# Stick-breaking attention: the running products alone go through the value product, and the values are shifted by one token through DRAM

## The chip, the cores and the metric

The kernel runs on one core of a Trainium2 chip. A time is the device time of one launch in microseconds (us), from the first instruction to the last; lower is better. The engines are PE (TensorE, matrix products), DVE (VectorE), ACT (ScalarE), POOL (GpSimd) and SP (SyncE, which here only issues DMAs). Each runs its own instructions strictly in the order in which they stand, and waits at the head of its queue until what the instruction needs has been signalled.

## The reference, cut to what matters

One layer of an encoder over 1024 tokens and 1024 channels: an RMS norm, a projection to four parts (pooling, q, k, v), a causal pooling mixer, stick-breaking attention with 8 heads of 64 channels, gates, an output projection, and an MLP. The change is in the attention:

```python
z = einsum('bhqd,bhkd->bhqk', qb, kb) * scale
mask = arange(t1)[None, :] < arange(t0, t1)[:, None]          # strictly causal: s < t
log_1mb = where(mask, log_sigmoid(-z), 0.0)
tail = cumsum(log_1mb, axis=3, reverse=True) - log_1mb
attn = where(mask, exp(log_sigmoid(z) + tail), 0.0)
out = einsum('bhqk,bhkd->bhqd', attn, vb)
```

So A[t,s] = sigmoid(z_ts) times the product of sigmoid(-z_tj) over s < j < t. With S[t,s] for the product of sigmoid(-z_tj) over s <= j < t, and S = 1 for s >= t, this is a difference of neighbours: A[t,s] = S[t,s+1] - S[t,s].

## The kernel before, in words

Everything is in float32 precision: an operand is split in a rounded high part and a rest (`hi`, `lo`), and a product is three matmuls (`mm3`, lines 115 to 117; 113 is the first of them where it is pinned behind an attention instruction). The program is written as one stream; a scheduler then sets the order of each engine's queue, and tile pools (memory that is handed on) set which instruction must wait for which.

`phase_in` normalises x, makes the pooling part (`pool_group` on DVE, `pool_mix` with a small product `dm` on PE, ACT line 427, DVE line 428, and two stores `yscr<-win` and `yscr<-u` by POOL), and the q and k of heads 0 and 1. Its work tiles lie in a pool `in_b`, which is released at its end.

`phase_attention` then takes over that memory for its pools `att` (the rows T, the split `ahi`, `alo`) and `att_s` (`self.sp`, small staging tiles). For each head, `att_scores` makes eight rows of 128 queries, from the widest (1024 keys) to the narrowest, in pieces of up to 512 keys: scores `z` in one of three PSUM buffers, F = sigmoid(-z) and T = sigmoid(z) by ACT (565, 566), a causal mask on T by POOL (568), a running product of F from right to left by DVE (574), and T times the neighbouring F by DVE (578). `att_steps` transposes T (591) in blocks, splits it by ACT and DVE (599, 600), and multiplies with the values (616) into the PSUM tile `o`; every value tile holds, per head, 64 channels of hi and 64 of lo, so the two halves of `o` are added at the end (625 by ACT, 627 by DVE).

Between these PE works off fillers, pieces of other jobs: gates (`dg`), later q and k (`dqk`), and the values (`dv`, `job_v`, 24 matmuls per tile of 128 tokens, first for heads 0 to 3 as soon as head 0 begins, tokens from the last tile to the first; then for heads 4 to 7 during heads 3 and 4, first tile to last). All fillers share two PSUM buffers (`dps`, tag `d`), in the order written: tile n needs the buffer of tile n-2 back. A value tile's buffer is given back when ACT (508) and DVE (509) have written the value tile in SBUF, which has a pool of its own (`vp`).

DMAs issued by SP load weights (line 79), one weight ahead, and make the swapped copies of q (485). POOL stores the gates and adds up weights for the MLP in DRAM (`wscr`).

Of the kernel before, what the change touches and what calls it, by code (L numbers as in the profile page):

```python
# [52 lines left out]
class Block:  # L53
# [118 lines left out]
    def build(self):  # L172
        tc, nc = self.tc, self.nc
# [315 lines left out]
    def job_v(self, grp):  # L489
        nc = self.nc  # L490
        w = [self.weights(("v", grp, j), 1 - j) for j in range(2)]

        for t in range(NK) if grp else range(NK - 1, -1, -1):
# [12 lines left out]
            dd = d[:, :256].rearrange("p (h x) -> p h x", h=4)  # L506
            r = self.rcol[:, t : t + 1]
            nc.scalar.activation(v[:, :, 0:64], dd, AF.Copy, scale=r)
            nc.vector.scalar_tensor_tensor(
                out=v[:, :, 64:128], in0=dd, scalar=r, in1=v[:, :, 0:64].bitcast(F32), op0=ALU.mult, op1=ALU.subtract  # L510
            )
            self.v[(grp, t)] = v

    def job_gate(self, i, h):
        nc = self.nc
# [22 lines left out]
    def att_scores(self, h, i):  # L538

        nc = self.nc
        p, j = h // 2, h % 2
        q, qs, k = self.qk[("q", p)][j], self.qk[("qs", p)][j], self.qk[("k", p)][j]
        w = (i + 1) * P
        tl = self.tp.tile([P, w], F32, name="T", tag=f"T{i}", bufs=1)
        f = self.tp.tile([P, 1024], F32, name="F", tag="F", bufs=1)
        tt = slice(i * P, i * P + P)  # L550
        past = self.past[:, 1024 - w :]

        low = min(H, w - 2 * P) if w > H else 0
        for c, n in ((low, w - low), (0, low)):
            if n == 0:
                continue
            top = c == low
            cols = slice(c, c + max(256, n))
            z = self.zps.tile([P, H], F32, name="z", tag="z", bufs=3)
            zz = z[:, : max(256, n)]  # L560
            m = nc.tensor.matmul(zz, q[:, tt], k[:, cols], start=True, stop=False)  # L561
# [3 lines left out]
            nc.scalar.activation(f[:, c : c + n], z[:, :n], AF.Sigmoid, scale=-1.0)  # L565
            nc.scalar.activation(tl[:, c : c + n], z[:, :n], AF.Sigmoid)
            if top:
                self.masked = nc.gpsimd.affine_select(  # L568
                    out=tl[:, w - P : w], in_=tl[:, w - P : w], pattern=[[-1, P]], compare_op=ALU.is_gt, fill=0.0,
                    base=0, channel_multiplier=1,  # L570
                )

            fr = f[:, c : c + n][:, ::-1]
            nc.vector.tensor_tensor_scan(  # L574
                fr, fr, past[:, c : c + n][:, ::-1], 1.0 if top else f[:, c + n : c + n + 1], ALU.mult, ALU.max
            )
            e = c + n - top
            nc.vector.tensor_mul(tl[:, c:e], tl[:, c:e], f[:, c + 1 : e + 1])  # L578
        return tl

    def att_steps(self, h, g, a):

        nc = self.nc
        o = self.zps.tile([P, H], F32, name="o", tag="o", bufs=1)
        for s in range(4 * g + 4):
            r0 = max(0, s - 4 * g)
            at = self.zps.tile([P, H], F32, name="at", tag="at", bufs=2)
            hi = self.tp.tile([P, H], F32R, name="ahi", tag="ahi", bufs=2)
            lo = self.tp.tile([P, H], F32R, name="alo", tag="alo", bufs=2)
            for r in range(r0, 4):  # L590
                t = nc.tensor.transpose(at[:, r * P : r * P + P], a[r][:, s * P : s * P + P], self.eye)  # L591
            self.marks.append(t)
            self.pump(self.w_out)

            c0, c = min(r0, 2) * P, r0 * P
            if r0 == 3:
                nc.gpsimd.memset(hi[:, c0:c].bitcast(F32), 0.0)
                nc.gpsimd.memset(lo[:, c0:c].bitcast(F32), 0.0)
# [3 lines left out]
            self.pending = (h, g, s, o, hi, lo, c0)  # L602
            yield

    def att_products(self):

        nc = self.nc
        if self.pending is None:
            return
        h, g, s, o, hi, lo, c0 = self.pending  # L610
        self.pending = None
        last = s == 4 * g + 3
        hd = (h % 4) * P
        v = self.v[(h // 4, s)].rearrange("p h x -> p (h x)")[:, hd : hd + P]
        for part in (hi, lo):
            t = nc.tensor.matmul(  # L616
                o[:, c0:], v, part[:, c0:], start=s == 0 and part is hi, stop=last and part is lo
            )
        self.marks.append(t)
        if not last:  # L620
            return
        b = 64 * (h % 2)
        for c in (0, 256):
            u = self.sp.tile([P, 256], F32, name="ou", tag="ou", bufs=1)
            nc.scalar.copy(u[64:128, :], o[64:128, c : c + 256])
            at = slice(g * H + c, g * H + c + 256)
            nc.vector.tensor_add(self.oT[h // 2][b : b + 64, at], o[0:64, c : c + 256], u[64:128, :])
# [18 lines left out]
    def phase_attention(self):  # L646
        tc, nc = self.tc, self.nc
# [9 lines left out]
        out = None  # L657
        for h in range(8):
# [9 lines left out]
            for n_row, i in enumerate(ROWS):  # L668
# [723 lines left out]
```

## Time and profile before

| what | value |
|---|---|
| median of 3 runs (lowest to highest) | 1276.06 us (1275.58 to 1276.24) |
| span of the profiled execution | 1274.1 us |
| median less that span | 2.0 us |
| PE busy | 1266.1 us, 99% |
| DVE busy | 924.9 us, 73% |
| ACT busy | 614.6 us, 48% |
| POOL busy | 169.6 us, 13% |

The page has no time of its own for the profiled execution beside its span; what the runs are longer by is start and end around it. A busy PE is a PE with a matmul somewhere in its pipeline: a matmul of 512 columns is listed with 389 ns and the next one starts some 225 ns later, so a pause of up to 0.16 us between two starts does not show as idle time. Attention, with its fillers, lies between about 77 and 450 us of the span.

### The profile page before, as it was taken

To read this page: it belongs to the slowest core of one execution; us is meant where nothing else is said; L and a number is where in the kernel's file an instruction comes from. 1 tells how busy PE (TensorE), PEld (TensorE's weight loads), DVE (VectorE), ACT (ScalarE), POOL (GpSimd) and SP (SyncE) were. 2 spreads that over 40 slices of the span, in tenths; PEclk is the share of its full clock that TensorE was granted. 3 is DMA by queue.
4 is the path that set the end of the run, shared out by engine and by line. 5 is a ranking of instruction groups with operands and counts; after the bars stand their busy time and mean duration, and the time that the engine had idled before them with its cause. 6 is when DMAs were issued, how large, how long until landed. Compare 5 with 4: busy or idle time off the path is not lost.

```text
span 1274.1 us, 16614 instructions
## 1 busy us (share of the span) xinstructions
PE 1266.1 (99%) x6043; PEld 1057.7 (83%) x6043; DVE 924.9 (73%) x1315; ACT 614.6 (48%) x1022; POOL 169.6 (13%) x314
## 2 busy tenths in 40 slices
PE   9999999999999999999999999999999999999998
PEld 6898888889888888888878888888888888888887
DVE  8787688786878747551777988877775655776975
ACT  8235455564555542232456646455454433344452
POOL 1002213221223121100101002212120000001000
PEclk9999999999999999999999999999999999999999
DMA  6254447694686138671529578656559546556551
GB/s 226 67 165 166 146 161 163 138 219 141 124 215 223 67 120 232 198 219 33 182 85 303 183 247 277 219 198 208 199 205 346 193 154 223 189 179 238 199 220 67
DMA packets 75729, 233.70 MB, mean 183 GB/s; under 512 B 8608, under 2 KB 11168, under 8 KB 73472
## 3 DMA queue, kind: packets, MB, share of 16 engines
q1 hardware_dynamic: 48352, 144.04, 33.9%
q0 software_dynamic: 27152, 88.49, 23.7%
q8 instruction: 47, 0.77, 0.2%
q14 instruction: 34, 0.28, 0.1%
q10 hardware_dynamic: 144, 0.13, 0.0%
HBM read 178.10 MB, written 83.89 MB: 206 GB/s over the span
## 4 chain that ended last, share of the span: by engine, by line
PE 94%; DVE 3%; issue 1%; ACT 1%; DMA 1%; POOL 0%; SPq 0%; DVEq 0%; ACTq 0%; POOLq 0%
PE d L116 20%; PE d L117 20%; PE d L115 20%; PE dg L117 4%; PE dg L116 4%; PE dg L113 4%; PE o L616 3%; PE at L591 2%; PE dqk L116 2%; PE dqk L117 2%; PE dqk L113 1%; PE z L564 1%; PE z L561 1%; DVE F L574 1%; PE dv L117 1%
## 5 line engine op out<-in xcount | busy, mean ns | idle before, releaser
L116 PE MATMUL d<-blo,whi 128*128 128x512 f32 (+1 forms) x456 | 172.3, 378 | 0.0
L117 PE MATMUL d<-bhi,wlo 128*128 128x512 f32 (+1 forms) x456 | 171.9, 378 | 0.0
L115 PE MATMUL d<-bhi,whi 128*128 128x512 f32 (+1 forms) x456 | 168.7, 378 | 0.0
L574 DVE TENSOR_TENSOR_SCAN F<-F,past 128x256 f32<-128x256 f32 (+2 forms) x96 | 94.2, 981 | 20.9 <-ACT F L565 20.0
L85 ACT CAST whi<-wraw 128x512 fp32r<-128x512 f32 (+1 forms) x88 | 67.7, 799 | 77.2 <-PE d L116 38.0
L113 PE MATMUL dg<-hT_hi,whi 128*128 128x512 f32 x253 | 101.7, 402 | 0.0
L117 PE MATMUL dg<-hT_hi,wlo 128*128 128x512 f32 x256 | 100.8, 394 | 0.0
L116 PE MATMUL dg<-hT_lo,whi 128*128 128x512 f32 x256 | 100.4, 392 | 0.0
L117 PEld LDWEIGHTS d<-bhi,wlo 128*128 128x128 f32 x456 | 85.8, 188 | 15.9
L116 PEld LDWEIGHTS d<-blo,whi 128*128 128x128 f32 x456 | 85.7, 188 | 15.9
L115 PEld LDWEIGHTS d<-bhi,whi 128*128 128x128 f32 x456 | 85.5, 188 | 16.1
L86 DVE TENSOR_TENSOR wlo<-wraw,whi 128x512 fp32r<-128x512 f32 (+1 forms) x88 | 77.7, 905 | 28.4 <-ACT whi L85 28.3
L116 PE MATMUL d<-b_lo,whi 128*128 128x512 f32 x196 | 76.2, 390 | 0.4 <-DVE b_lo L836 0.4
L115 PE MATMUL d<-b_hi,whi 128*128 128x512 f32 x196 | 75.6, 389 | 0.0
L565 ACT ACTIVATE F<-z 128x256 f32<-128x256 f32 (+2 forms) x96 | 47.2, 493 | 58.8 <-DVE T L578 34.4
L117 PE MATMUL d<-b_hi,wlo 128*128 128x512 f32 x196 | 74.7, 389 | 0.0
L1124 DVE TENSOR_TENSOR wlo<-slots_hi,whi 128x1024 fp32r<-128x1024 f32 x29 | 35.5, 1225 | 53.1 <-ACT whi L1122 53.1
L600 DVE TENSOR_TENSOR alo<-at,ahi 128x512 fp32r<-128x512 f32 (+1 forms) x96 | 52.0, 553 | 29.9 <-ACT ahi L599 28.8
L1122 ACT CAST whi<-slots_hi 128x1024 fp32r<-128x1024 f32 x29 | 30.5, 1052 | 84.5 <-PE d L116 71.5
L599 ACT CAST ahi<-at 128x512 fp32r<-128x512 f32 (+1 forms) x96 | 45.1, 482 | 47.4 <-PE at L591 44.0
L1122 ACT CAST whi<-slots_lo 128x1024 fp32r<-128x1024 f32 x27 | 28.4, 1053 | 73.4 <-PE d L116 59.7
L578 DVE TENSOR_TENSOR T<-T,F 128x255 f32<-128x255 f32 (+3 forms) x96 | 53.1, 556 | 11.0 <-POOL T L568 2.5
(323 smaller groups left out, 3309.3 us busy)
## 6 DMA issues: line engine op xcount, KB each, us to landing
wraw<-w SPq DMA_DIRECT2D x80, 512.0 KB, 4.3
wscr<-w POOLq DMA_DIRECT2D x24, 1024.0 KB, 10.0
ext_b<-ascr SPq DMA_DIRECT2D x40, 512.0 KB, 4.3
gscr<-gs POOLq DMA_DIRECT2D x32, 256.0 KB, 4.2
gate<-gscr POOLq DMA_DIRECT2D x16, 512.0 KB, 4.5
pscr<-p SPq DMA_DIRECT2D x32, 256.0 KB, 3.2
braw<-w SPq DMA_DIRECT2D x16, 512.0 KB, 5.1
ascr<-c POOLq DMA_DIRECT2D x32, 256.0 KB, 5.0
```

Of the source, the lines that this page charges most:

```text
L85: nc.scalar.copy(hi[:, c], raw[:, c])
L86: self.last_lo = nc.vector.tensor_sub(lo[:, c], raw[:, c], hi[:, c].bitcast(F32)).ins
L113: nc.tensor.matmul(ps, wh, rh, start=first and i == 0, stop=False)
L115: nc.tensor.matmul(ps, wh, rh, start=first and i == 0, stop=False)
L116: nc.tensor.matmul(ps, wh, rl, start=False, stop=False)
L117: nc.tensor.matmul(ps, wl, rh, start=False, stop=last and i == n - 1)
L565: nc.scalar.activation(f[:, c : c + n], z[:, :n], AF.Sigmoid, scale=-1.0)
L574: nc.vector.tensor_tensor_scan(fr, fr, past[:, c : c + n][:, ::-1], 1.0 if top else f[:, c + n : c + n + 1], ALU.mult, ALU.max)
L578: nc.vector.tensor_mul(tl[:, c:e], tl[:, c:e], f[:, c + 1 : e + 1])
L599: nc.scalar.copy(hi[:, c:], at[:, c:])
L600: nc.vector.tensor_sub(lo[:, c:], at[:, c:], hi[:, c:].bitcast(F32))
L1122: last_split[0] = nc.scalar.copy(hi, src).ins
```

## The change: what it does

`att_scores` makes only sigmoid(-z), straight into the row T, and runs the product over it in place. The second sigmoid, the mask and the multiplication with the neighbour are gone, and F with them. The rows that are transposed now hold S instead of A; masked places hold 1.

The difference is moved to the values: over a row of keys up to the end E of its block, sum of A[t,s] v[s] = v[E-1] + sum of S[t,s] (v[s-1] - v[s]), with v[-1] = 0. `job_v` therefore evicts a value tile with one ACT instruction to a staging tile `vs` (from `att_s`, 2 buffers), SP stores it to DRAM (`vscr`, one zero row ahead of token 0), and `v_steps` loads the same tile shifted by one token (`vb`, 2 buffers), subtracts on DVE, and splits on ACT and DVE. The load of tile t needs the stores of tiles t and t-1; for the first group, which runs from the last tile to the first, `v_steps` of tile t+1 is written behind the eviction of tile t. v[E-1] (`vlast`, 64 channels of 8 heads for 8 blocks) is gathered by four DMAs of single values per group, and is added as the bias of the eviction of `o`, which is cut in halves for that. POOL sets the first token's output to zero. The weight sums are issued two at a time behind POOL's memsets instead of one every second row.

```diff
+        self.vlast = cp.tile([P, 8, NK], F32, name="vlast")
+        nc.vector.memset(self.pad, 0.0)
+        self.vscr = dp.tile([1 + P * NK, H], F32, name="vscr")
+        nc.sync.dma_start(self.vscr[0:1, :].rearrange("o (p n) -> (o p) n", p=P), self.pad[:, 0:4])
...
-            v = self.vp.tile([P, 4, P], F32R, name=f"v{grp}_{t}", tag="v", bufs=9)
-            dd = d[:, :256].rearrange("p (h x) -> p h x", h=4)
-            r = self.rcol[:, t : t + 1]
-            nc.scalar.activation(v[:, :, 0:64], dd, AF.Copy, scale=r)
-            nc.vector.scalar_tensor_tensor(
-                out=v[:, :, 64:128], in0=dd, scalar=r, in1=v[:, :, 0:64].bitcast(F32), op0=ALU.mult, op1=ALU.subtract
-            )
-            self.v[(grp, t)] = v
+            s = self.sp.tile([P, 256], F32, name="vs", tag="vs", bufs=2)
+            nc.scalar.activation(s, d[:, :256], AF.Copy, scale=self.rcol[:, t : t + 1])
+            nc.sync.dma_start(self.vscr[1 + t * P : 1 + t * P + P, cols], s)
+            if grp:
+                self.v_steps(grp, t, s)
+            else:
+                if t < NK - 1:
+                    self.v_steps(grp, t + 1, later)
+                later = s
+        if not grp:
+            self.v_steps(grp, 0, later)
+        for h in range(4 * grp, 4 * grp + 4):
+            nc.sync.dma_start(
+                self.vlast[64:128, h, :], self.vscr[P : P * NK + 1 : P, 64 * h : 64 * h + 64].rearrange("i d -> d i")
+            )
+
+    def v_steps(self, grp, t, s):
+        b = self.sp.tile([P, 256], F32, name="vb", tag="vb", bufs=2)
+        nc.sync.dma_start(b, self.vscr[t * P : t * P + P, 256 * grp : 256 * grp + 256])
+        nc.vector.tensor_sub(b, b, s)
+        bb = b.rearrange("p (h x) -> p h x", h=4)
+        v = self.vp.tile([P, 4, P], F32R, name=f"v{grp}_{t}", tag="v", bufs=9)
+        nc.scalar.copy(v[:, :, 0:64], bb)
+        nc.vector.tensor_sub(v[:, :, 64:128], bb, v[:, :, 0:64].bitcast(F32))
+        self.v[(grp, t)] = v
...
-            nc.scalar.activation(f[:, c : c + n], z[:, :n], AF.Sigmoid, scale=-1.0)
-            nc.scalar.activation(tl[:, c : c + n], z[:, :n], AF.Sigmoid)
-            if top:
-                self.masked = nc.gpsimd.affine_select(
...
-            fr = f[:, c : c + n][:, ::-1]
+            f = tl[:, c : c + n]
+            nc.scalar.activation(f, z[:, :n], AF.Sigmoid, scale=-1.0)
             nc.vector.tensor_tensor_scan(
...
-            e = c + n - top
-            nc.vector.tensor_mul(tl[:, c:e], tl[:, c:e], f[:, c + 1 : e + 1])
...
-            nc.scalar.copy(u[64:128, :], o[64:128, c : c + 256])
+            for j in (0, P):
+                i = (g * H + c + j) // P
+                nc.scalar.activation(
+                    u[64:128, j : j + P], o[64:128, c + j : c + j + P], AF.Identity, bias=self.vlast[64:128, h, i : i + 1]
+                )
...
+        if g == 0:
+            nc.gpsimd.memset(self.oT[h // 2][b : b + 64, 0:1], 0.0)
```

The scheduler's order moves with it. PE has the same number of matmuls, 6033 rows with and without the change. Three places follow, where heads 0 to 3 get their values; line numbers of the changed program are up to 24 higher (565 becomes 589, 427 becomes 431, 421 becomes 425).

On ACT, from the third pooling group to the first sigmoids. `v0_7` is the value tile of tokens 896 to 1023, `v0_6` the one before it; `win` and `ph` belong to the pooling. Before:

```order
L421 CAST ph_742<-win_699 128x1024
L508 ACTIVATE v0_7_924<-dv_899,rcol_165 128x4x64
L508 ACTIVATE v0_6_952<-dv_927,rcol_165 128x4x64
L427 ACTIVATE win_699<-dm_746,vt_150 128x512
L427 ACTIVATE win_699<-dm_752,vt_150 128x512
L508 ACTIVATE v0_5_998<-dv_955,rcol_165 128x4x64
L421 CAST ph_814<-win_769 128x1024
L508 ACTIVATE v0_4_1026<-dv_1001,rcol_165 128x4x64
L508 ACTIVATE v0_3_1054<-dv_1029,rcol_165 128x4x64
L427 ACTIVATE win_769<-dm_818,vt_150 128x512
L427 ACTIVATE win_769<-dm_824,vt_150 128x512
```

The same place in the changed program (`vs_922`, `vs_950`, `vs_995`, `vs_1029` are the evictions of tiles 7, 6, 5 and 4):

```order
L425 CAST ph_818<-win_773 128x1024
L431 ACTIVATE win_773<-dm_822,vt_150 128x512
L431 ACTIVATE win_773<-dm_828,vt_150 128x512
L589 ACT_TABLE_LOAD
L589 ACTIVATE T_878<-z_879 128x512
L589 ACTIVATE T_878<-z_884 128x512
L511 ACTIVATE vs_922<-dv_897,rcol_165 128x256
L511 ACTIVATE vs_950<-dv_925,rcol_165 128x256
L589 ACTIVATE T_984<-z_985 128x384
L589 ACTIVATE T_984<-z_990 128x512
L589 ACTIVATE T_1097<-z_1098 128x256
L534 CAST v0_7_956<-vb_953 128x4x64
```

The evictions of tiles 7 and 6 stood ahead of the last pooling group; they now stand behind it, behind the table load and behind the first two sigmoids. The next eviction (`vs_995`) stands behind the cast of the finished tile 7, and so on down to tile 0: one cast, one eviction.

On PE, just behind the last matmul of `dv` for tile 6. Before:

```order
L561 MATMUL z_982<-k0_776,q0_637 128x384
L564 MATMUL z_982<-k0_776,qs0_736 128x384
L116 MATMUL dm_746<-pq_743,wmh_519 128x512
L117 MATMUL dm_746<-ph_742,wml_520 128x512
L116 MATMUL dm_752<-pq_743,wmh_519 128x512
L117 MATMUL dm_752<-ph_742,wml_520 128x512
L115 MATMUL dv_955<-whi_779,hT_hi1_291 128x256
```

Now:

```order
L117 MATMUL dm_756<-ph_746,wml_524 128x512
L115 MATMUL dm_822<-ph_818,wmh_523 128x512
L115 MATMUL dm_828<-ph_818,wmh_523 128x512
L116 MATMUL dm_822<-pq_819,wmh_523 128x512
L117 MATMUL dm_822<-ph_818,wml_524 128x512
L116 MATMUL dm_828<-pq_819,wmh_523 128x512
L117 MATMUL dm_828<-ph_818,wml_524 128x512
L584 MATMUL z_990<-k0_780,q0_641 128x512
L587 MATMUL z_990<-k0_780,qs0_740 128x512
L584 MATMUL z_1098<-k0_780,q0_641 128x256
L587 MATMUL z_1098<-k0_780,qs0_740 128x256
L115 MATMUL dv_959<-whi_783,hT_hi1_295 128x256
```

The matmuls of the last pooling group and two score pieces now stand between `dv` of tile 6 and of tile 5; before, three tiles of `dv` (72 matmuls) came first. Further on, the remaining score pieces of head 0, three pieces of head 1 and 16 transposes stand between the tiles of `dv`, and all of them stand ahead of the first gate.

On SP, the same group of values. Before, weights and the copies of q alone stood here; now:

```order
L512 DMA vscr_168<-vs_922 128x256
L512 DMA vscr_168<-vs_950 128x256
L530 DMA vb_953<-vscr_168 128x256
L512 DMA vscr_168<-vs_995 128x256
L530 DMA vb_998<-vscr_168 128x256
L512 DMA vscr_168<-vs_1029 128x256
L530 DMA vb_1032<-vscr_168 128x256
L512 DMA vscr_168<-vs_1063 128x256
L530 DMA vb_1066<-vscr_168 128x256
```

Store and load alternate, each load one tile behind the last store.

More of the change, by code (lines that the diff above doesn't have):

```diff
@@ L491, in job_v @@
         w = [self.weights(("v", grp, j), 1 - j) for j in range(2)]
+        cols = slice(256 * grp, 256 * grp + 256)
         for t in range(NK) if grp else range(NK - 1, -1, -1):
@@ L504, in job_v @@
                     yield
-            v = self.vp.tile([P, 4, P], F32R, name=f"v{grp}_{t}", tag="v", bufs=9)
-            dd = d[:, :256].rearrange("p (h x) -> p h x", h=4)
-            r = self.rcol[:, t : t + 1]
-            nc.scalar.activation(v[:, :, 0:64], dd, AF.Copy, scale=r)
-            nc.vector.scalar_tensor_tensor(
-                out=v[:, :, 64:128], in0=dd, scalar=r, in1=v[:, :, 0:64].bitcast(F32), op0=ALU.mult, op1=ALU.subtract
-            )
-            self.v[(grp, t)] = v
+            s = self.sp.tile([P, 256], F32, name="vs", tag="vs", bufs=2)
[12 more added lines that the diff above has]
+                self.vlast[64:128, h, :], self.vscr[P : P * NK + 1 : P, 64 * h : 64 * h + 64].rearrange("i d -> d i")
+            )
+    def v_steps(self, grp, t, s):
+        nc = self.nc
+        b = self.sp.tile([P, 256], F32, name="vb", tag="vb", bufs=2)
[6 more added lines that the diff above has]
+        self.v[(grp, t)] = v
     def job_gate(self, i, h):
@@ L548, in att_scores @@
         tl = self.tp.tile([P, w], F32, name="T", tag=f"T{i}", bufs=1)
-        f = self.tp.tile([P, 1024], F32, name="F", tag="F", bufs=1)
         tt = slice(i * P, i * P + P)
@@ L564, in att_scores @@
             nc.tensor.matmul(zz, qs[:, tt], k[:, cols], start=False, stop=True)
-            nc.scalar.activation(f[:, c : c + n], z[:, :n], AF.Sigmoid, scale=-1.0)
-            nc.scalar.activation(tl[:, c : c + n], z[:, :n], AF.Sigmoid)
-            if top:
-                self.masked = nc.gpsimd.affine_select(
-                    out=tl[:, w - P : w], in_=tl[:, w - P : w], pattern=[[-1, P]], compare_op=ALU.is_gt, fill=0.0,
-                    base=0, channel_multiplier=1,
-                )
-            fr = f[:, c : c + n][:, ::-1]
+            f = tl[:, c : c + n]
+            nc.scalar.activation(f, z[:, :n], AF.Sigmoid, scale=-1.0)
             nc.vector.tensor_tensor_scan(
-                fr, fr, past[:, c : c + n][:, ::-1], 1.0 if top else f[:, c + n : c + n + 1], ALU.mult, ALU.max
-            )
-            e = c + n - top
-            nc.vector.tensor_mul(tl[:, c:e], tl[:, c:e], f[:, c + 1 : e + 1])
+                f[:, ::-1], f[:, ::-1], past[:, c : c + n][:, ::-1], 1.0 if top else tl[:, c + n : c + n + 1],
+                ALU.mult, ALU.max,
+            )
         return tl
@@ L597, in att_steps @@
                 nc.gpsimd.memset(hi[:, c0:c].bitcast(F32), 0.0)
-                nc.gpsimd.memset(lo[:, c0:c].bitcast(F32), 0.0)
+                self.zeroed = nc.gpsimd.memset(lo[:, c0:c].bitcast(F32), 0.0)
             nc.scalar.copy(hi[:, c:], at[:, c:])
@@ L602, in att_steps @@
             self.pending = (h, g, s, o, hi, lo, c0)
+            if s == 4 * g + 3 and h < 7:
+                with self.tc.issue_after(self.zeroed.ins):
+                    next(self.wsums)
+                    next(self.wsums)
             yield
@@ L672, in phase_attention @@
                 self.pump(w_in * share[n_row])
-                if h < 7 and n_row % 2:
-                    with tc.issue_after(self.masked.ins):
-                        next(self.wsums)
                 if h == 0 and n_row < 4:
```

## The prediction

> **What bounds the kernel now.** I read the page first (busy shares, then the chain that ended last), then what PE waited for, then PE's pace in the attention beside a stage of plain matmuls.
>
> ```profile
> PE 1266.1 (99%) x6043; PEld 1057.7 (83%) x6043; DVE 924.9 (73%) x1315; ACT 614.6 (48%) x1022; POOL 169.6 (13%) x314
> PE 94%; DVE 3%; issue 1%; ACT 1%; DMA 1%; POOL 0%; SPq 0%; DVEq 0%; ACTq 0%; POOLq 0%
> ...
> PE at L591 <- DVE T L578: 0.4, 1, 0.4
> ...
> PE o L616 <- DVE oT L627: 0.4, 1, 0.4
> ...
> 100.00:450.00 350.00, 348.85 (x1849) 296.94 (x1849) 275.56 (x433) 195.69 (x422) 82.83 (x156) 1.00 0.59 160
> 500.00:550.00 50.00, 50.00 (x222) 41.40 (x221) 29.80 (x42) 10.86 (x14) 8.50 (x12) 1.00 0.73 196
> ...
> L113 PE MATMUL dg<-hT_hi,whi 128*128 128x512 f32 x253 | 101.7, 402 | 0.0
> L115 PE MATMUL d<-bhi,whi 128*128 128x512 f32 x408 | 155.6, 389 | 0.0
> ```
>
> PE is 94% of the chain. In 350 us of attention it idles 1.15 us (350.00 - 348.85) and waits for the softmax engines for 0.4 us at a time. What short pauses hide in its busy time is seen in the means: the pinned gate matmul is listed 402 ns where plain ones have 389, 13 ns x 253 = 3.3 us. Allowing as much again for `dqk` and the products, all that faster DVE, ACT and POOL work can give back is 0 to 8 us. PE's matmuls are the same in number and shape after the change, so the time can only fall by these pauses, and rises by every new wait of PE.
>
> **What is removed.**
>
> ```profile
> L566 ACT ACTIVATE T<-z x96: 271/504/625, 102.5 to 448.2; 128x512 f32<-128x512 f32 x40, 128x384 f32<-128x384 f32 x24, 128x256 f32<-128x256 f32 x24, 128x128 f32<-128x128 f32 x8
> L578 DVE TENSOR_TENSOR T<-T,F 128x255 f32<-128x255 f32 (+3 forms) x96 | 53.1, 556 | 11.0 <-POOL T L568 2.5
> L568 POOL TENSOR_SCALAR_AFFINE_SELECT T<-T 128x128 f32<-128x128 f32 x64 | 34.8, 544 | 168.9 <-ACT T L566 156.8 <-PE o L616 6.4 <-PE dqk L117 5.6
> L625 ACT COPY ou<-o 64x256 f32<-64x256 f32 x32 | 11.8, 368 | 13.0 <-PE o L616 8.5 <-DVE oT L627 3.9
> ```
>
> 96 x 0.504 = 48 us of ACT, 53 us of DVE, 35 us of POOL; 64 half evictions for 32 cost ACT some 6 us back (64 x 0.28, estimated from 0.368 for twice the width, less 11.8). All of it runs beside PE. I credit 1.5 us of the 0 to 8.
>
> **What is added where the first values are made.** This term carries the sum. ACT, DVE and PE in that stretch, from the timeline:
>
> ```profile
> 84.58 1.22 DVE L405 TENSOR_TENSOR win<-win 128x1022 f32<-128x1022 f32 x1 [1.40 <-DMA yscr<-win]
> 91.64 0.17 DVE L413 TENSOR_TENSOR win<-win,u 128x16 f32<-128x16 f32 x1
> 91.84 1.05 ACT L421 CAST ph<-win 128x1024 fp32r<-128x1024 f32 x1 [1.84 <-DVE win L413]
> 92.91 1.23 DVE L422 TENSOR_TENSOR pq<-win,ph 128x1024 fp32r<-128x1024 f32 x1 [1.11 <-ACT ph L421]
> ...
> 85.36 0.48 ACT L508 ACTIVATE v<-dv,rcol 128x256 fp32r<-128x256 f32 x1 [3.71 <-PE dv L117]
> 96.21 1.27 ACT L427 ACTIVATE win<-dm,vt 128x512 fp32r<-128x512 f32 x2 [0.45 <-PE dm L117]
> 100.73 1.28 ACT L565 ACT_TABLE_LOAD   x1 [0.72 <-DMA yscr<-win]
> 102.03 0.60 ACT L565 ACTIVATE F<-z 128x512 f32<-128x512 f32 x1
> ...
> 85.16 0.34 PE L561 MATMUL z<-k,q 128*128 128x384 f32 x1
> 86.44 0.28 PE L115 MATMUL dv<-whi,hT_hi 128*128 128x256 f32 x1
> 94.96 0.28 PE L117 MATMUL dv<-whi,hT_lo 128*128 128x256 f32 x1
> 95.08 0.63 PE L115 MATMUL dm<-ph,wmh 128*128 128x512 f32 x2
> 122.50 0.60 PE L591 MATMUL at<-eye,T 128*128 128x128 f32 x4
> ```
>
> Before, tiles 7 and 6 are evicted by 85.8. In the changed order their evictions stand behind the table load, which waits for the last pooling store, and two sigmoids. PE now comes to the last `dm` without the 72 `dv` (86.44 to 95.08, 0.12 us each) ahead of it, so that `dm` follows its operands: DVE has two value instructions less on the way, `ph` from about 91.3, `pq` done at 93.6, L427 at 94.2 instead of 96.21. All behind it is 2.0 us earlier: table load 98.7, sigmoids 100.05 to 101.1, evictions of tiles 7 and 6 done at 102.0.
>
> From there every eviction waits for a round trip: eviction, store, load, subtraction, cast, next eviction (two staging buffers, and ACT's order).
>
> ```profile
> L508 ACT ACTIVATE v<-dv,rcol 128x256 fp32r<-128x256 f32 x16 | 7.7, 479 | 12.3 <-PE dv L117 12.1
> L509 DVE SCALAR_TENSOR_TENSOR v<-dv,rcol,v 128x256 fp32r<-128x256 f32 x16 | 7.6, 477 | 3.8 <-ACT v L508 3.8
> out<-ff SPq DMA_DIRECT2D x13, 128.0 KB, 1.8
> pscr<-p SPq DMA_DIRECT2D x32, 256.0 KB, 3.2
> wraw<-w SPq DMA_DIRECT2D x80, 512.0 KB, 4.3
> ...
> L79 SPq DMA_DIRECT2D wraw<-w x4: 327/328/328, 33.0 to 56.1; - x4
> ...
> DMA to landing us min/median/max: 3.4/3.4/3.5
> ```
>
> Eviction and cast 0.48 each, subtraction 0.48. The store is 128 KB like `out<-ff`: 1.8 (upper bound 2.3, between it and twice the size). A load of 128 KB is not in the trace: between 1.8 (the store of its size) and 3.4 (four times the size, alone on the queue); I take 2.2, nearer to the equal size. Four hand-overs, some 0.2. Period 0.48 + 1.8 + 2.2 + 0.48 + 0.48 + 0.2 = 5.6. Six periods lead from tile 6 to tile 0, and in one of them three running products and two splits stand ahead of the subtraction on DVE, +0.8: tile 0 is evicted at 102.0 + 33.6 + 0.8 = 136.4.
>
> The second gate tile needs that buffer. PE's work from 85.16 until there, all in front of it: 144 `dv` x 0.12 = 17.3; 10 `dm` x 0.23 = 2.3 (512 columns: 50 us / 222); 13 score pieces, two matmuls each by their columns, 4.6; 16 transposes at most 0.15 each by the last row above, I take 1.5; the first gate tile, 24 x 0.226 = 5.4. Sum 31.1, so 116.3 without waits. PE waits 136.4 - 116.3 = **20 us**. Nothing covers it: what PE could do instead needs the same two PSUM buffers or the same three score buffers. The products with the last values stand 54 gate matmuls further on (12 us); those values need a last round trip of about 7 us, and PE does not wait for them again. Period 5.0 (load 1.8, no hand-overs) gives 16 us, period 7.3 (load 3.4, store 2.3) 30 us.
>
> By the Trainium skill, "DMA: Bandwidth & Descriptors", section "Anatomy of one DMA — SWDGE (gpsimd) path", a DMA costs about 2.0 us plus its bytes at 436 GB/s, by which store and load would be 2.3 each and the wait about 24 us; the store row above (1.8) is already below it.
>
> **The other added terms.** *Start.* A store of the zero row stands second on SP.
>
> ```profile
> 1.24 0.42 SPq L280 DMA_DIRECT2D vt<-vec  x1
> 3.94 0.18 DVE L281 TENSOR_SCALAR gn<-vt 128x32 f32<-128x32 f32 x1 [2.49 <-DMA vt<-vec]
> ```
>
> Every first load is one issue later, +0.4 (0 to 0.8). *Values of heads 4 to 7.* Here two tiles are in flight (two stores, two loads), so a pair takes about 6.2.
>
> ```profile
> L113 PE MATMUL dv<-whi,hT_hi x64: 278/283/368, 274.2 to 304.3; 128*128 128x256 f32 x64
> wscr<-w POOLq DMA_DIRECT2D x24, 1024.0 KB, 10.0
> SPq L79 <- DVE wlo L86: 454.2, 47, 32.2
> ```
>
> PE spends 30 us on these eight tiles, 7.5 a pair: hidden at 2.2 per load. With the 1 MB sums on the same DMA engines a load may take the 4.3 of the weights, a pair 8.3, and DVE and ACT hold the next rows up while they wait: 0 to 6, I take 1.5. *`vlast`, weight sums, zeroed token.* SP waits 454 us for DVE before weight loads, so a few issues more are hidden; `vlast` lands some 20 us ahead of its first use. 0.
>
> **Sum.** 20 + 0.4 + 1.5 - 1.5 = 20.4 on the profiled span of 1274.1, 1294.5; the median lies 2.0 above that span: **1296 us**.
>
> **Rivals.**
> (A) *The round trip is hidden by an early start.* If the evictions of tiles 7 and 6 kept their place (85.8), six periods would end at 120.2, 4 us of waiting: 1276 + 0.4 + 4 = 1280. For it: the data are there at 85.4. Against: ACT's queue has them behind the table load. 7%.
> (B) *The relief of DVE and ACT wins: faster.* Price: up to 8 us less, in the pauses between pinned matmuls of attention; it decides only if the wait stays below them, which needs (A) and a period under 6: 1276 + 4 - 8 = 1272. Against: PE's waits for these engines are 0.4 us. 4%. The case in between, no change because PE hides both: 3%.
> (C) *PE resumes at a lower pace after each pause.*
>
> ```profile
> 1.43 4.02 PE L313 MATMUL idle<-zero 128*128 128x512 bf16 x9 [1.43 <-DVE zero L310]
> 0.00:5.00 5.00, 3.57 (x9) 1.20 (x9) 0.75 (x5) 2.52 (x4) 3.80 (x9) 1.00 0.64 167
> ```
>
> The nine dummy matmuls at the start take 0.45 us each, against 0.225 later for as many columns, though the granted clock stands at 1.00 in both. If PE fell to half pace in the pauses (5.7 us behind the last `dm`, 2.7 per period), its 28 us of work from 100.7 on would take up to 56 and end near 157 instead of 136: 1317, or 1307 if half of it runs so. Against: the DMA chain leaves PE idle for part of that stretch, which absorbs part of it. 10%. The Trainium skill says so in "TensorE: Matmul & The Clock Gate", section "Part 1: The HAM clock gate": after an idle window of about 3.4 us PE runs at half rate until it was busy for as long; by that rule (C) would come in part.
>
> **How the numbers follow.** Forecast (a wait of 14 to 31 us) 76%, (A) 7%, (B) 4%, no change 3%, (C) 10%. Range 1285 to 1313: the period's bounds (16 and 30) with the small terms (-6 to +7); left out are (A), (B), no change and the upper part of (C), 18%. What a measurement here can tell from no change is about 0.2%, 2.5 us: faster 4%, same 3%, slower 93%.
>
> **What would show it.** Right: PE idle some 20 us between 86 and 137, in pauses ended by ACT's `vs` and by the sigmoid behind the table load; L511 evictions at about 102 and then every 5.6 us; `vb<-vscr` landing in about 2.2; PE in 140 to 450 paced as before. Wrong: `vs` of tiles 7 and 6 evicted near 85; PE idle below 10 us there; waits in the second group of the same size; or a loss spread over all heads.

## The result, and the profile after

The changed kernel takes 1312.59 us (median, 1310.51 to 1313.52); the kernel before, run beside it, 1275.82. The ratio is 1.0285, 95% interval 1.027 to 1.030: slower by 36.8 us. The forecast was 1296. The profiled execution spans 1308.8 us, 34.7 more than that of before, and 14.3 more than the 1294.5 of the sum.

The page of the changed kernel, busy times and chain:

```profile
PE 1277.0 (98%) x6043; PEld 1065.3 (81%) x6043; DVE 881.2 (67%) x1236; ACT 591.9 (45%) x974; POOL 136.0 (10%) x258
PE 92%; DMA 4%; DVE 2%; ACT 1%; issue 1%; SPq 0%; ACTq 0%; DVEq 0%; POOLq 0%
```

DVE is 44 us lighter, ACT 23, POOL 34, on as many matmuls, and none of it shortens the chain. DMA has gone from 1% to 4% of it. What PE waited for, in the changed kernel (us in total, times, longest):

```profile
PE dv L113 <- ACT vs L511: 8.6, 2, 6.5
PE z L584 <- ACT T L589: 5.9, 1, 5.9
PE dm L115 <- ACT ph L425: 5.5, 1, 5.5
PE du L115 <- ACT hT_hi L329: 2.9, 2, 1.6
PE dg L115 <- ACT vs L511: 1.6, 1, 1.6
```

Before, its longest wait for another engine in attention was 0.4. By stretch, first the changed kernel, then the one before (window; its length, then busy us of PE, PEld, DVE, ACT and POOL, each with its instructions; granted clock, the share of full speed that PE's clock was given; DMA share; GB/s):

```profile
0.00:25.00 25.00, 20.34 (x65) 13.59 (x66) 17.34 (x35) 18.92 (x35) 4.97 (x10) 0.86 0.84 287
75.00:150.00 75.00, 61.60 (x356) 53.65 (x355) 44.16 (x72) 26.80 (x52) 4.28 (x8) 0.89 0.36 112
300.00:350.00 50.00, 41.42 (x273) 38.81 (x272) 26.63 (x46) 19.82 (x49) 5.07 (x7) 0.90 0.77 163
500.00:550.00 50.00, 50.00 (x224) 41.48 (x223) 29.54 (x40) 15.98 (x22) 8.95 (x15) 1.00 0.70 199
```

```profile
0.00:25.00 25.00, 22.90 (x88) 15.83 (x89) 20.72 (x38) 21.54 (x40) 5.42 (x10) 1.00 0.81 288
75.00:150.00 75.00, 74.62 (x437) 65.64 (x437) 51.67 (x80) 37.31 (x73) 14.55 (x26) 1.00 0.42 151
300.00:350.00 50.00, 50.00 (x268) 42.71 (x267) 38.26 (x62) 28.02 (x61) 11.03 (x20) 1.00 0.61 148
```

Three stretches lose, and in all three PE both pauses and has a clock below 1.00. To have pauses and slow matmuls in one number, I take PE's *loss* in a stretch: over all matmuls that start in it, the time to the next start, less the median of that time for the same operand shape in the kernel before, summed; then what the kernel before has in the stretch is taken off. The changed kernel loses 4.9 us in 0 to 25, 17.6 in 75 to 150 (values of heads 0 to 3), 11.7 in 300 to 350 (values of heads 4 to 7) and 0.3 in all the rest: 34.5 of the 34.7 by which its span is longer.

### The profile page after: what moved, and what is told of

Read it like the earlier page. It is cut to its first block, busy times and chain, and to the rows that moved or that the text cites. A ratio compares the mean times of both kernels' runs of the same rounds, so it can differ in the third digit from the quotient of the medians.

```text
span 1308.8 us, 16417 instructions
## 1 busy us (share of the span) xinstructions
PE 1277.0 (98%) x6043; PEld 1065.3 (81%) x6043; DVE 881.2 (67%) x1236; ACT 591.9 (45%) x974; POOL 136.0 (10%) x258
## 3 DMA queue, kind: packets, MB, share of 16 engines
q1 hardware_dynamic: 57328, 148.25, 34.5%
## 4 chain that ended last, share of the span: by engine, by line
PE 92%; DMA 4%; DVE 2%; ACT 1%; issue 1%; SPq 0%; ACTq 0%; DVEq 0%; POOLq 0%
PE d L117 20%; PE d L116 20%; PE d L115 20%; PE dg L113 4%; PE dg L117 4%; PE dg L116 4%; PE o L635 3%; PE dqk L116 2%; PE dqk L117 2%; PE at L606 2%; PE dqk L113 2%; DMA vb<-vscr 1%; DMA vscr<-vs 1%; PE z L584 1%; PE z L587 1%
## 5 line engine op out<-in xcount | busy, mean ns | idle before, releaser
L590 DVE TENSOR_TENSOR_SCAN T<-T,past 128x256 f32<-128x256 f32 (+2 forms) x96 | 92.8, 974 | 38.8 <-ACT T L589 35.3
L589 ACT ACTIVATE T<-z 128x256 f32<-128x256 f32 (+2 forms) x96 | 44.7, 493 | 44.4 <-PE z L587 42.3
L1146 DVE TENSOR_TENSOR wlo<-slots_lo,whi 128x1024 fp32r<-128x1024 f32 x27 | 33.0, 1222 | 35.5 <-ACT whi L1144 35.3
## 6 DMA issues: line engine op xcount, KB each, us to landing
wscr<-w POOLq DMA_DIRECT2D x24, 1024.0 KB, 10.2
```

What stands on the lines that cost most here:

```text
L589: nc.scalar.activation(f, z[:, :n], AF.Sigmoid, scale=-1.0)
L590: nc.vector.tensor_tensor_scan(f[:, ::-1], f[:, ::-1], past[:, c : c + n][:, ::-1], 1.0 if top else tl[:, c + n : c + n + 1], ALU.mult, AL ...
L1146: last_split[1] = nc.vector.tensor_sub(lo, src, hi.bitcast(F32)).ins
```

## The experiments

The loss in us by stretch and the medians of all runs. The matmuls on zeros that one run adds at the start are counted in its loss there.

| kernel | 0-25 | 75-150 | 300-350 | median us | ratio to before (95%) |
|---|---|---|---|---|---|
| changed kernel | 4.9 | 17.6 | 11.7 | 1312.6 | 1.0285 (1.027-1.030) |
| zero row stored late | 0.0 | 19.8 | 11.1 | 1308.4 | 1.0254 (1.0237-1.0271) |
| zero row in two pieces | 2.9 | 17.9 | 10.9 | 1311.1 | 1.0267 (1.0252-1.0282) |
| more matmuls on zeros | 3.5 | 18.4 | 12.7 | 1310.7 | 1.0266 (1.0250-1.0281) |
| before, with the zero row | 4.8 | 0.0 | -0.1 | 1279.7 | 1.0026 (1.0016-1.0037) |
| one pair of sums moved | 3.8 | 18.3 | 5.1 | 1303.6 | 1.0213 (1.0197-1.0228) |
| both pairs moved | 4.7 | 20.8 | -0.3 | 1299.9 | 1.0189 (1.0174-1.0205) |
| staging in its own space | 3.6 | 12.3 | 12.2 | 1303.8 | 1.0215 (1.0198-1.0232) |
| loads ready | 3.5 | 14.8 | -0.3 | 1293.8 | 1.0141 (1.0126-1.0156) |
| own space, loads ready | 4.4 | -0.7 | -0.1 | 1278.4 | 1.0017 (1.0007-1.0026) |
| light softmax, no shift | 1.1 | -0.3 | -0.1 | 1275.1 | 0.9992 (0.9982-1.0001) |
| before, difference on the rows | -0.1 | 0.0 | -0.1 | 1275.2 | 0.9991 (0.9983-1.0000) |
| three edits together | -0.1 | 11.6 | -0.1 | 1286.8 | 1.0083 (1.0069-1.0097) |

Where an edit does not touch a stretch, its loss there still varies from kernel to kernel: 17.6 to 20.8 in 75 to 150, 10.9 to 12.7 in 300 to 350, 3.5 to 4.9 at the start with the zero row in its place. Each loss is that of one profiled execution. So differences of up to 3 us in the second column, and of up to 2 in the other two, mean nothing.

### The start

The rows behind the 4.9. First DVE, ACT and PE in the changed kernel (start, us, engine and line; in brackets the idle time before it and what ended it), then the same two steps of the kernel before:

```profile
5.72 0.53 DVE L285 TENSOR_SCALAR gn<-vt 128x32 f32<-128x32 f32 x1 [4.25 <-DMA vt<-vec]
7.07 0.50 PE L115 MATMUL du<-hT_hi,whi 128*128 128x512 f32 x1 [1.59 <-ACT hT_hi L329]
9.12 0.72 ACT L329 ACTIVATE hT_hi<-x,gn 128x512 fp32r<-128x512 f32 x1 [2.11 <-DMA x<-x]
```

```profile
5.35 0.53 PE L115 MATMUL du<-hT_hi,whi 128*128 128x512 f32 x1
5.63 0.72 ACT L325 ACTIVATE hT_hi<-x,gn 128x512 fp32r<-128x512 f32 x1 [0.34 <-DMA x<-x]
```

The vector and x come late, PE starts 1.7 us later, and waits again for the second x. DMAs issued in the first 4 us, with the median to landing, changed kernel and then before:

```profile
x<-x SPq DMA_DIRECT2D x3, 256.0 KB, 6.9
wraw<-w POOLq DMA_DIRECT2D x3, 128.0 KB, 6.1
vscr<-pad SPq DMA_DIRECT2D x1, 2.0 KB, 4.1
```

```profile
x<-x SPq DMA_DIRECT2D x3, 256.0 KB, 3.9
wraw<-w POOLq DMA_DIRECT2D x3, 128.0 KB, 4.8
```

And PE's pace, in the window from 8 to 14 us, changed kernel and then before:

```profile
8.00:14.00 6.00, 4.67 (x11) 3.06 (x12) 4.13 (x9) 4.88 (x11) 0.00 (x0) 0.59 1.04 396
```

```profile
8.00:14.00 6.00, 6.00 (x26) 4.54 (x25) 6.00 (x13) 6.00 (x13) 0.00 (x0) 1.00 1.05 413
```

Eleven matmuls instead of 26: behind the second pause starts are 0.43 us apart until 15.6, and 0.23 from there on.

**The store of the zero row behind the first loads.**

```diff
         self.vscr = dp.tile([1 + P * NK, H], F32, name="vscr")
-        nc.sync.dma_start(self.vscr[0:1, :].rearrange("o (p n) -> (o p) n", p=P), self.pad[:, 0:4])
...
         for t, src in zip((self.eye, self.rcnt), self.consts):
             nc.sync.dma_start(t, src)
+        nc.sync.dma_start(self.vscr[0:1, :].rearrange("o (p n) -> (o p) n", p=P), self.pad[:, 0:4])
```

> The changed kernel, with the store of the zero row issued behind all loads of the start instead of second on SP. Theory (the store of 128 pieces of 16 bytes holds up every first load by 1 to 1.3 us and PE's first matmul by 1.7, and PE then runs at a granted clock of 0.5 from 9.0 to 15.9): the first x and vector loads land in 2.9 and 2.7 us again, no half clock before 20 us, 5 us less, about 1307.5. Rival (the store costs its issue alone, the 0.4 of the prediction): 0.4 us less, 1312.2.

Measured: a loss of 0.0 at the start, PE at full pace from 8.3, 1308.4. The window from 8 to 14 us of this kernel:

```profile
8.00:14.00 6.00, 6.00 (x26) 4.78 (x27) 6.00 (x13) 6.00 (x13) 0.00 (x0) 1.00 1.05 409
```

The whole term goes with the place of this one DMA of 2 KB.

**The store alone, added to the kernel before.**

```diff
+        nc.vector.memset(self.pad, 0.0)
+        self.vscr = dp.tile([1 + P * NK, H], F32, name="vscr")
+        nc.sync.dma_start(self.vscr[0:1, :].rearrange("o (p n) -> (o p) n", p=P), self.pad[:, 0:4])
```

> The kernel before with nothing added but the store of the zero row, second on SP (128 pieces of 16 bytes). Theory (this store alone makes the loss at the start, by late loads and the half pace that PE keeps until it has been busy long enough): PE's first real matmul near 7.1 instead of 5.35, pace 0.43 until 14 to 16 us, 4 to 5 us slower, about 1280.5. Rival (one issue more, 0.4; the rest of the loss came from elsewhere in the change): 1276.5.

Measured: 4.8 lost at the start and nothing elsewhere, 0.26% slower (0.16 to 0.37%). Nothing else of the change takes part in this term.

**As two pieces of 1 KB.**

```diff
-        nc.sync.dma_start(self.vscr[0:1, :].rearrange("o (p n) -> (o p) n", p=P), self.pad[:, 0:4])
+        nc.sync.dma_start(self.vscr[0:1, :].rearrange("o (p n) -> (o p) n", p=2), zero[0:2, :].bitcast(F32))
```

> The changed kernel with the same zero row at nearly the same place of SP's queue (behind the first load), as two pieces of 1 KB instead of 128 of 16 bytes. If the number of small pieces is what delays the loads: 4 to 5 us less, about 1308. If any further DMA there, or its issue, delays them: 0 to 0.5 us less.

Measured: 2.9 instead of 4.9. The vector landed in 2.7 us and PE's first matmul came at 5.37, as before; then the second x and the weights were late (x a median of 5.7 us instead of 3.9, the weights from POOL's queue 5.1 instead of 4.8), PE paused once more for each, and ran at the slow pace from 9.45 to 12.6. It lies between both theories. The store had also come to stand third on SP, behind the vector, so place and number of pieces are not told apart; what it is in the store that delays the loads stays open.

**Fourteen matmuls on zeros instead of nine.**

```diff
-        for _ in range(9):
+        for _ in range(14):
```

> The changed kernel with 14 instead of 9 matmuls on zeros at the start, so that PE is busy until about 7 us, when the first real matmul comes. Theory (of the 5 us at the start, 1.7 are late loads and the rest is the half clock, which follows PE's pause from 5.6 to 7.1): granted clock 1.0 until 20 us, 3 to 3.5 us less, about 1309.3. Rival (the 5 us are late loads alone): no change, 1312.6.

Measured: 3.5 lost at the start instead of 4.9, and a median 1.9 below that of the changed kernel, with ranges that overlap. The expected 3 to 3.5 us did not come in full, if they came at all. PE did reach full pace at 6.5 us, but then paused for the second x (starts at 8.21, 9.53, 10.35) and fell back to 0.43 us from 10.9 to 13.5. The late loads come first and the slow pace follows them, so warming PE ahead of them brought 1 to 2 us at most.

### The values of heads 4 to 7

PE and DVE of the changed kernel, and the DMAs issued from 300 to 336 us, then from 330 to 336:

```profile
315.29 0.39 PE L113 MATMUL dv<-whi,hT_hi 128*128 128x256 f32 x1 [2.04 <-ACT vs L511]
329.69 0.58 PE L113 MATMUL dv<-whi,hT_hi 128*128 128x256 f32 x1 [6.54 <-ACT vs L511]
328.40 0.42 DVE L531 TENSOR_TENSOR vb<-vb,vs 128x256 f32<-128x256 f32 x1 [6.85 <-DMA vb<-vscr]
```

```profile
wscr<-w POOLq DMA_DIRECT2D x4, 1024.0 KB, 13.0
vscr<-vs SPq DMA_DIRECT2D x6, 128.0 KB, 6.2
vb<-vscr SPq DMA_DIRECT2D x6, 128.0 KB, 5.3
```

```profile
vb<-vscr SPq DMA_DIRECT2D x2, 128.0 KB, 2.2
vscr<-vs SPq DMA_DIRECT2D x1, 128.0 KB, 1.7
```

The store and the load of one tile take 11.5 us beside the weight sums (four of 1 MB, issued two at a time), and 3.9 us behind them.

**One pair of sums moved.** The edit left out the sums of two places of the program; in the trace only the second pair (issued at 313.7) had come from them, the pair at 299.9 was still there.

```diff
-                    next(self.wsums)
-                    next(self.wsums)
+                    for _ in range({(3, 0): 0, (4, 1): 0}.get((h, g), 2 + (h > 4))):
+                        next(self.wsums)
```

> The changed kernel without the four weight sums (1 MB each, accumulated in DRAM) that POOL issues while the values of heads 4 to 7 are made; they are issued with the later heads instead, 28 as before. Theory (these DMAs make the value stores and loads 3 to 4 times as long, and that is the loss between 300 and 350 us): stores 1.7 and loads 2.1 there, PE's pause before the last value tile gone, clock 1.0, 11 to 12 us less, about 1301. Rival (the round trip with two tiles in flight is too slow by itself): 0 to 3 us less.

Measured: 5.1 lost there instead of 11.7, one pause of 4.0 us at 312.5; the stores issued behind 316 landed in 1.7. Half the cause away, and somewhat more than half of the loss.

**Both pairs moved** (the same edit with `(3, 1)` and `(3, 0)`).

> The changed kernel without both pairs of weight sums that POOL issues while the values of heads 4 to 7 are made (the pairs at 299.9 and 313.7; the run before this one had moved the second alone, and gained about half); 28 sums as before, the four come with heads 5 and 6. Theory (the 1 MB sums slow the value stores and loads threefold): all stores there 1.7 and loads 2.1, PE without a pause over 0.5 there, 11 to 12 us less than the changed kernel, about 1301. Rival (the first pair does no harm, as PE's first pause there was 2 us): no further gain, about 1303.5.

Measured: no loss there. The DMAs from 300 to 336 us of this kernel, and its window:

```profile
vscr<-vs SPq DMA_DIRECT2D x8, 128.0 KB, 1.7
vb<-vscr SPq DMA_DIRECT2D x8, 128.0 KB, 2.1
```

```profile
300.00:350.00 50.00, 50.00 (x341) 46.17 (x340) 33.59 (x59) 26.55 (x63) 4.28 (x12) 1.00 0.31 87
```

Without the sums the pair of tiles in flight is hidden, as the prediction had worked out for 2.2 per load. The first pair, alone in the run above, had cost 5.1, though PE's pause behind it is only 2.0 us in the changed kernel.

By the Trainium skill, "DMA: Bandwidth & Descriptors", section "Issuing engines are not separate DMA queues", DMAs interleave on the same 16 engines whichever engine issued them. These runs agree: sums issued by POOL made SP's store take 6.2 us instead of 1.7.

### The values of heads 0 to 3

ACT's evictions in the changed kernel:

```profile
104.52 1.28 ACT L589 ACT_TABLE_LOAD   x1 [3.27 <-DMA yscr<-win]
106.78 0.84 ACT L511 ACTIVATE vs<-dv,rcol 128x256 f32<-128x256 f32 x2
112.59 0.47 ACT L511 ACTIVATE vs<-dv,rcol 128x256 f32<-128x256 f32 x1
117.66 0.47 ACT L511 ACTIVATE vs<-dv,rcol 128x256 f32<-128x256 f32 x1
...
139.69 0.47 ACT L511 ACTIVATE vs<-dv,rcol 128x256 f32<-128x256 f32 x1
```

Tiles 7 and 6 at 107.6, then six periods of 5.4 to the eviction of tile 0. Two causes can stand behind the 17.6, the late first eviction and the period, and the next three runs take away the one, the other, and both.

**Staging tiles in the pool of the value tiles.** The evictions of tiles 7 to 4 come to stand ahead of the table load.

```diff
-            s = self.sp.tile([P, 256], F32, name="vs", tag="vs", bufs=2)
+            s = self.vp.tile([P, 256], F32, name="vs", tag="vs", bufs=2)
...
-        b = self.sp.tile([P, 256], F32, name="vb", tag="vb", bufs=2)
+        b = self.vp.tile([P, 256], F32, name="vb", tag="vb", bufs=2)
```

> The changed kernel with the staging tiles vs and vb in the pool of the value tiles, which is there from the start, instead of the attention's staging pool, which takes over memory that the pooling still uses; two buffers each, as in the changed kernel. The evictions of tiles 7 to 4 then stand ahead of the sigmoids' table load, and three periods of 5.4 are left from about 109.5. Theory (the late first eviction makes two thirds of the wait): tile 0 evicted near 126 where PE needs it at 121, PE's loss between 75 and 150 us 5 to 6 us instead of 17.6, about 1301. Rival (the round trip alone sets the wait, wherever it begins): 0 to 3 us less.

Measured: 12.3, twice what the theory left. ACT of this kernel, its DMAs from 121 to 136 us, and PE's longest wait in the stretch:

```profile
106.83 1.28 ACT L589 ACT_TABLE_LOAD   x1 [4.73 <-issue]
109.76 0.50 ACT L511 ACTIVATE vs<-dv,rcol 128x256 f32<-128x256 f32 x1
116.36 0.47 ACT L511 ACTIVATE vs<-dv,rcol 128x256 f32<-128x256 f32 x1
122.64 0.47 ACT L511 ACTIVATE vs<-dv,rcol 128x256 f32<-128x256 f32 x1
131.50 0.47 ACT L511 ACTIVATE vs<-dv,rcol 128x256 f32<-128x256 f32 x1
```

```profile
wraw<-w SPq DMA_DIRECT2D x2, 512.0 KB, 4.1
vscr<-vs SPq DMA_DIRECT2D x2, 128.0 KB, 4.3
```

```profile
PE z L584 <- ACT T L589: 4.1, 1, 4.1
```

The four tiles left have periods of 6.6, 6.3 and 8.9 instead of 5.4. In the last of them, with PE further on, two weight loads of 512 KB fall beside the store, which takes over 4 us instead of 1.7, and tile 0 is evicted at 131.5 instead of 126. The theory also left out a pause: PE still waited 4.1 us for the first sigmoid behind the table load, and the granted clock was 0.5 for 3.4 us behind it.

**Loads that wait for no store.**

```diff
-        nc.sync.dma_start(b, self.vscr[t * P : t * P + P, 256 * grp : 256 * grp + 256])
+        nc.sync.dma_start(b, self.w[O_V][:, 0:256])
```

> The changed kernel with vb loaded from a weight (128 KB, as many pieces) instead of the stored values, so that no load waits for a store; the shift of the values is left out by this, the stores stay. Theory (six periods of eviction, store, load, subtraction, cast): without the store's 1.7 a period is 3.4 to 4 us instead of 5.4, PE's loss between 75 and 150 us 6 to 9 us instead of 17.6; between 300 and 350 us, with the loads beside the weight sums but not behind the stores, 3 to 6 instead of 11.7; in all about 1296 to 1300. Rival (the late first eviction alone sets the wait): 0 to 3 us less.

Measured: 14.8 in 75 to 150, so the theory's 6 to 9 was wrong and the rival's 0 to 3 less was right. The eviction of tile 0 came at 125.7, 14 us earlier than in the changed kernel, and evictions now waited for PE. PE's waits in this kernel:

```profile
PE dm L115 <- ACT ph L425: 6.1, 1, 6.1
PE z L584 <- ACT T L589: 5.9, 1, 5.9
```

Two pauses ahead of the first eviction remain whole, and with the slow pace behind them (granted clock 0.5 for 13.7 us) they are the 14.8. So the changed kernel's 17.6 could not be had back by a shorter trip: 13.5 of it had gone by 106.46, when PE resumed behind its second pause, some 2.3 more went with the slow pace up to 111.4, and the waits for `vs` made up the rest (1.6 and 0.3 us).

In 300 to 350 nothing was lost, better than the theory said. The window of this kernel:

```profile
300.00:350.00 50.00, 50.00 (x319) 45.24 (x319) 33.06 (x55) 25.80 (x61) 5.82 (x12) 1.00 0.88 202
```

The four weight sums were still there (issued at 295.6 and 312.1, while the values were made from 292 to 322), and beside them the stores took 7.1 us and the loads 6.6, more than in the changed kernel. PE lost nothing all the same. So in heads 4 to 7 slow transfers alone cost nothing: the loss needs the sums and a load that waits for its store, and it is gone when either is taken away.

**Both together.**

> The changed kernel with both edits that were run alone: staging tiles in the pool of the value tiles (PE's loss between 75 and 150 us fell from 17.6 to 12.3), and vb loaded from a weight, so that no load waits for a store (14.8; the shift is left out by this). Theory now (late first evictions and the round trip are two limits of nearly the same height: with one gone the other still holds PE up): with both gone 0 to 3 us are lost there, none between 300 and 350 us, 3.5 to 5 at the start, about 1281 to 1284. Rival (the gains only add, 5.3 and 2.8 of 17.6): 9 to 10 us lost there, about 1289 or more.

Measured: -0.7 in 75 to 150, below the 0 to 3 of the theory. The window of this kernel:

```profile
75.00:150.00 75.00, 75.00 (x442) 66.15 (x441) 49.94 (x81) 33.20 (x63) 6.75 (x14) 1.00 0.44 138
```

One edit gave 5.3 us, the other 2.8 (no more than the stretch varies), both 18.3. The late first eviction and the round trip are two limits of nearly one height, and each hides what the other would give. The scheduler's order moved further, too: here seven of the eight evictions stand ahead of the table load, with the pool alone four. PE's wait for the sigmoid behind the table load (5.9 us in the changed kernel and with loads ready, 4.1 with the pool alone) is gone: PE has matmuls of `dv` to do in that time.

### The relief

**The light softmax without the shift.** Values are made as before, by the lines that the change removes from `job_v`.

```diff
-            s = self.sp.tile([P, 256], F32, name="vs", tag="vs", bufs=2)
...
+            nc.scalar.activation(v[:, :, 0:64], dd, AF.Copy, scale=r)
+            nc.vector.scalar_tensor_tensor(
+                out=v[:, :, 64:128], in0=dd, scalar=r, in1=v[:, :, 0:64].bitcast(F32), op0=ALU.mult, op1=ALU.subtract
+            )
...
-            for j in (0, P):
...
+            nc.scalar.copy(u[64:128, :], o[64:128, c : c + 256])
```

> The changed kernel's softmax (one sigmoid, one running product, no mask, no product with the neighbour) with the values made as in the kernel before: no stores, loads, differences or last values; the differences of neighbours are left out by this. It shows what the relief of ACT, DVE and POOL is worth alone. Theory (PE bounds the attention, relief 1.5 of 0 to 8): 1273 to 1276. Rival (the relief is large and is given back by the round trip): 1268 or less.

Measured: 1275.1 beside 1276.2, ratio 0.9992 (0.9982 to 1.0001). All that faster DVE, ACT and POOL work is worth here is 1.1 us, between -0.1 and 2.3.

**The difference on the rows.** The kernel before without the second sigmoid and the mask, and without moving values.

```diff
-            nc.scalar.activation(tl[:, c : c + n], z[:, :n], AF.Sigmoid)
-                self.masked = nc.gpsimd.affine_select(
...
+                self.masked = nc.gpsimd.memset(tl[:, w - 1 : w], 0.0)
...
-            nc.vector.tensor_mul(tl[:, c:e], tl[:, c:e], f[:, c + 1 : e + 1])
+            nc.vector.tensor_sub(tl[:, c:e], f[:, c + 1 : e + 1], f[:, c:e])
```

> The kernel before with the difference of neighbours taken on the row itself, on DVE: T = F one place to the right less F, in place of the second sigmoid, the mask (one column set to zero stays) and the product. It has the change's lighter ACT and POOL without moving the values. Theory (PE bounds the attention and the softmax engines are covered; the softmax without the shift gave a ratio of 0.9992): 0 to 1.5 us faster than before, 1274.5 to 1276. Rival (the pauses of 13 ns between pinned matmuls come from these engines, up to 8 us): 1270 to 1273.

Measured: 1275.2 beside 1276.1, ratio 0.9991 (0.9983 to 1.0000). ACT is 36 us lighter and POOL 28, and the time is at best a tenth of a per cent lower. It is the only whole kernel here that is not slower than the one before, and within what can be told from no change.

### The three edits together

The zero row late, both pairs of sums moved, staging in its own space.

> The changed kernel, whole, with the three edits that moved something: the zero row stored behind the first loads, both pairs of weight sums moved behind the values of heads 4 to 7, staging tiles in the pool of the value tiles. If the terms are separate (start 0, heads 0 to 3 12.3, heads 4 to 7 0): 1276 + 12 = 1288, between 1285 and 1291, still slower than the kernel before. If they hang together (later loads of weights then meet the stores elsewhere): above 1291.

Measured: 1286.8, losses -0.1, 11.6 and -0.1. The terms are separate. What is left is the values of heads 0 to 3, and with a relief of about 1 us there is nothing to set against it.

## Why the prediction was right and wrong

**Direction: right, by its first reason.** PE bounds the attention and the relief is covered: credited with 1.5 us, measured at about 1 without the shift. In the changed kernel, the stretches outside the three sum to +0.3, so the credit did not show there.

**Heads 0 to 3: the size right by its rule, 20 against 17.6, the pauses not those that it named.** Of the named pauses the one behind the last `dm`, before the sigmoid behind the table load, came (5.9, forecast 5.7). The pauses of 2.7 in every period, ended by `vs`, did not: PE waited 1.9 us in all for `vs`. Instead it waited 5.5 us for `ph`, ahead of the last `dm`; the step has `dm` follow its operands there, but gives this wait no size. Between 86 and 137 PE idled 13.1 us and not some 20, and about 4 us went with the slow pace (8.3 us of running at a granted clock of 0.5), which the step put at nothing and left to rival (C).

The chain itself was forecast well. Less the 4.9 of the start, the evictions of tiles 7 and 6 end at 102.7 (forecast 102.0), the period is 5.4 (5.6), tile 0 is evicted at 135.3 (136.4). The store took 1.7 (1.8) and the load 2.1 (2.2); the 2.3 for each, an estimate from a fit for DMAs issued by GpSimd in the Trainium skill, "DMA: Bandwidth & Descriptors", section "Anatomy of one DMA — SWDGE (gpsimd) path", is above both, and the measurement decides. The rule, end of the chain less PE's work, gave the right size, and PE did come to the second gate tile as the chain ended: it waited 0.3 us there. But it came so late by its own pauses, and with the trip shortened it still lost 14.8. That a second limit, which the step did not see, lay at nearly the same height is luck for the forecast.

**The start: the sum's first mis-sized term, 0.4 (0 to 0.8) against 4.9.** It priced the store as one more issue. The loads behind and beside it landed up to 3 us later, and PE, which before has one gap of 1.2 us there and is at full pace from 9.2, ran at half pace until 15.6.

**Heads 4 to 7: the second, 1.5 (0 to 6) against 11.7.** Here the step failed at its upper bound: beside the sums a load was allowed the 4.3 of a weight load, and the store nothing. Measured were 6.2 for the store and 5.3 for the load, and both stand in the trip. It spoke of the sums as work on the same DMA engines, but took its price from the median of all 80 weight loads. The trace of before had a nearer row, the DMAs issued from 251 to 277 us there:

```profile
wscr<-w POOLq DMA_DIRECT2D x3, 1024.0 KB, 10.6
wraw<-w SPq DMA_DIRECT2D x2, 512.0 KB, 7.1
```

Beside these sums and four copies of q, a weight load took 7.1 instead of 4.3. (From 290 to 330, beside one sum, it took 5.2, so which row to take is easier to say afterwards.) Read by stretch, this would have raised both transfers, where the step raised one to 4.3. One of the signs of being wrong came in part: PE idled 8.6 us in this group, two thirds of what it idled in the first.

**The sum.** 4.5 too little at the start, 10.2 in heads 4 to 7, 1.5 of relief that did not show, 0.5 elsewhere, less 2.4 in heads 0 to 3: the 14.3 by which the span is longer than forecast. The median lay 3.8 above the span instead of 2.0, as the profiled execution was the shortest of the four (1310.5). So the time came out at the upper edge of the range, by two terms that the range had counted with 7 us together and that made 16.6. That it lay inside at all is luck: the room came from heads 0 to 3, where the range allowed 30 and 17.6 were lost.

**The rivals.** (A) needed early evictions: made early by a pool, they left a loss of 12.3 and not the 4 worked out, since PE still waited 4.1 us for the sigmoid behind the table load and the last periods grew to between 6.3 and 8.9, the longest with weights loaded beside it. (B) has no price to live on: the relief is about 1 us. (C) came in part. The granted clock was 0.5 for 17 us in heads 0 to 3, but PE stood idle for half of that time (8.8 us), and the stretch lost less than forecast. (Its 1307 does not follow from its own numbers: 28 us of work from 100.7 on, half of it at half pace, end at 142.7, 6 us behind 136.4, which gives 1302.) That the time lies in (C)'s 1307 to 1317 is owed to the other two terms, of which the start is (C)'s mechanism at another place. The case for it is stronger than the 10% said: in the changed kernel a granted clock of 0.5 follows every pause of 2.0 us or more.

## What to carry to other kernels

A DMA that is put into a stretch and waited for must be priced beside what else is in flight there, stores as well as loads: a store of 128 KB took 1.7 us alone, 4.3 beside two weight loads and 6.2 beside sums of 1 MB. If nothing waits for store and load in turn, the same slowness can cost nothing: with the loads made ready, stores of 7.1 us did not hold PE up. Where two waits end at nearly the same time, removing one gives little, so a kernel with both removed is needed before either is called harmless. Taking work off engines that the bound engine never waits for is worth about its pauses, here 1 us for 96 sigmoids and as many products, so any new wait of the bound engine decides the sign.

## What the runs showed of the hardware

PE's pace has two values here, 0.43 and 0.23 us for 512 columns, and the granted clock of the changed kernel falls to 0.5 for 6.8 us at the start, for 17.1 from 94.4, and for 3.4 and 6.8 between 316 and 333: whole multiples of 3.4. By the Trainium skill, "TensorE: Matmul & The Clock Gate", section "Part 1: The HAM clock gate (the "warmup" mystery)", the lower clock is the default, it is left and entered by windows of about 3.4 us that run freely, and 512 columns take 426.7 ns in it. The traces agree with the pace and with the steps: the stretches at full clock between those at 0.5 are multiples of 3.4 too (78.5 and 204.8 us). They do not agree with the idle window of about 3.4 us that the prediction takes from that section: the clock also fell behind a pause of 2.0 us, for one step. The free-running window may be why the same store costs 3.5 to 4.9 us in different kernels, which no run here tests.

The granted clock in the rows can miss the first slow stretch. In the kernel with one pair of sums moved, the window from 8 to 14 us shows 12 matmuls at a clock of 1.00, where the kernel before has 26:

```profile
8.00:14.00 6.00, 5.70 (x12) 3.70 (x13) 4.65 (x10) 5.41 (x12) 0.00 (x0) 1.00 1.06 404
```

PE started there every 0.43 us up to 14.2, and the recorded clock changes begin at about that time. The count of matmuls in a window is the safer reading.

I had not expected that a store of 2 KB, in 128 pieces of 16 bytes, would cost 4 to 5 us at the start; that is shown by its place and by adding it alone. What in it delays the loads is not.
